# Seven block products for 15 of 22 up-projection pairs in one SwiGLU phase, and modulation tiles moved to the other three

## The chip, the cores and the metric

The kernel runs on one core of one Trainium2 chip. The metric is the device time of one execution in microseconds. TensorE is called PE here, VectorE DVE, ScalarE ACT, GpSimd POOL and SyncE, which issues the weight transfers, SP.

## What is computed

Two layers of a diffusion backbone over 256 latent and 256 context tokens, D = 1024. Each layer is a half-step SwiGLU, a token mixer and a second half-step SwiGLU; each of them is modulated with shift, scale and gate and wrapped in a layer norm. What matters here:

```python
def modulate(h, shift, scale): return h * (1.0 + scale) + shift
def post_norm(h, y, gate, res_w, g, b):
    return layer_norm(ALPHA * h + res_w * gate * y, g, b)
def swiglu(u, w_up, w_down):
    a, v = jnp.split(u @ w_up, 2, axis=-1)          # D_FF = 2816 columns each
    return (jax.nn.silu(a) * v) @ w_down
def ffn_sublayer(h, m, j, w_up, w_down, g, b):
    u = modulate(h, m[:, :, 3 * j], m[:, :, 3 * j + 1])
    return post_norm(h, swiglu(u, w_up, w_down), m[:, :, 3 * j + 2], FFN_RES_W, g, b)
...
m_lat = (s_lat @ w_ada[l] + b_ada[l])               # 9 modulation vectors per layer, for latents
m_ctx = (s_ctx @ w_ada[l] + b_ada[l])               # and for context
```

## The kernel before

Activations lie transposed, 128 channels on the partitions and all 512 tokens along a row (context in the left 256, latents in the right), so u is eight pages, each as a high part (uh, fp32r) and a low part (ul); two pages share a tile, hence the names u0 to u3. Every product is three fp32r matmuls (`mm3`, L370): high by high (L372), high by low (L373), low by high (L374).

Weights arrive in chunks of 512 KB, eight blocks of 128x128, in an order fixed beforehand. SP issues the transfer into one of three raw buffers wr (L255); ACT copies it into the high part wh (L342); DVE subtracts for the low part wl (L344). There are three split slots wh/wl. A chunk feeds 24 matmuls. A slot comes free when PE has used it; then ACT's next copy can begin.

The phases are called (layer, sub-layer): (0,0) is the first SwiGLU, (0,2) the second of layer 0, (1,0) the first of layer 1, which the change is about, and (1,2) the last, on the 256 latents alone. A SwiGLU phase (`ffn`) has an up projection of 22 pairs ft, a chunk of a and one of v, 24 matmuls each into a bank of 512. The first two pairs (three in (0,0)) are made while the layer norm before them brings the u pages one by one (`k_outer`, `ln_apply`: L676 makes u, L677 its low part). `act` takes a pair from the banks: silu on ACT (L760), product on DVE (L761), high part on ACT (L764), low part on DVE (L765). The hidden pages r are kept split. The down projection goes over eight output blocks, the last two in halves of the tokens (`tail`), so that the layer norm of half 0 overlaps with PE's work on half 1; L560 adds a finished block into the residual.

The modulation vectors are not made on PE: `ada_part` takes a 512 KB tile of w_ada through the same raw buffers, and DVE multiplies and accumulates it with two broadcast rows (L488, twice per tile) and adds the bias (L492). 128 tiles are spread over the SwiGLU phases, one in the middle of each chunk of the up projections and two per block of the down projections: 50 in (0,0), 52 in (0,2), 26 in (1,0).

Each engine executes its instructions in the order of a scheduler that works from the program's dependencies. Dependencies on a PSUM bank are kept for the bank as a whole.

## Time and profile before

| | us |
|---|---|
| median of three executions | 2721.28 |
| lowest, highest | 2720.58, 2723.74 |
| the profiled execution | 2722.64 |
| its span on the core | 2720.7 |
| PE busy in the span | 2659.9 |
| DVE busy | 1928.3 |
| ACT busy | 1222.9 |

The span is what the profiler sees from the first to the last instruction; 1.9 us of the execution lie around it. In the trace (0,0) runs from about 50 to 391 us, (0,2) from 1208 to 1577, (1,0) from 1577 to 1947 (its layer norm to 1603, its up projection to about 1822), and the last phase from 2507 to the end. The mixers lie between. In a timeline a row is one instruction or a run of equal ones: start, duration, engine, line, operation, output and inputs, shape, count; in brackets the idle time ahead of it and what ended it.

### The profile page before, as it was taken

To read this page: it belongs to the slowest core of one execution; us is meant where nothing else is said; L and a number is where in the kernel's file an instruction comes from. 1 tells how busy PE (TensorE), PEld (TensorE's weight loads), DVE (VectorE), ACT (ScalarE), POOL (GpSimd) and SP (SyncE) were. 2 spreads that over 40 slices of the span, in tenths; PEclk is the share of its full clock that TensorE was granted. 3 is DMA by queue.
4 is the path that set the end of the run, shared out by engine and by line. 5 is a ranking of instruction groups with operands and counts; after the bars stand their busy time and mean duration, and the time that the engine had idled before them with its cause. 6 is when DMAs were issued, how large, how long until landed. Compare 5 with 4: busy or idle time off the path is not lost.

```text
span 2720.7 us, 38673 instructions
## 1 busy us (share of the span) xinstructions
PE 2659.9 (98%) x14869; PEld 2280.2 (84%) x14869; DVE 1928.3 (71%) x3469; ACT 1222.9 (45%) x1755; POOL 353.8 (13%) x296
## 2 busy tenths in 40 slices
PE   9999999999999999999999999999998999999998
PEld 7888897778887888888888888888977898899997
DVE  5788769599877545468887588633697998676654
ACT  4323237963345344433323142332388745574543
POOL 0000132112121000040000130001312112012002
PEclk9999999999999999999999999999999999999999
DMA  7666534134343222235666446532333354343563
GB/s 280 193 189 200 172 122 130 60 99 149 105 134 109 78 86 78 88 99 170 194 195 191 132 129 199 169 120 97 108 123 105 111 174 150 107 142 124 175 191 116
DMA packets 117833, 380.49 MB, mean 140 GB/s; under 512 B 13888, under 2 KB 22352, under 8 KB 117648
## 3 DMA queue, kind: packets, MB, share of 16 engines
q1 hardware_dynamic: 116000, 373.52, 42.5%
q0 software_dynamic: 1504, 4.34, 0.5%
q8 instruction: 116, 1.90, 0.3%
q14 instruction: 69, 0.57, 0.1%
q10 hardware_dynamic: 144, 0.17, 0.0%
HBM read 373.63 MB, written 4.33 MB: 139 GB/s over the span
## 4 chain that ended last, share of the span: by engine, by line
PE 56%; DVE 7%; ACT 3%; issue 2%; DMA 1%; POOL 0%; SPq 0%; POOLq 0%; DVEq 0%; ACTq 0%
PE bank L372 17%; PE bank L373 17%; PE bank L374 17%; PE bank L1282 1%; PE bank L1262 1%; DVE wl L344 1%; DVE x L869 1%; DMA wr<-in_ws_dram 1%; DMA x<-acs_d 1%; DVE f L669 0%; DVE m1l L344 0%; ACT wh L342 0%; PE bank L921 0%; DVE f L670 0%; DVE f L676 0%
## 5 line engine op out<-in xcount | busy, mean ns | idle before, releaser
L342 ACT ACTIVATE wh<-wr 128x1024 fp32r<-128x1024 f32 x388 | 410.2, 1058 | 727.1 <-PE bank L373 493.2
L344 DVE TENSOR_TENSOR wl<-wr,wh 128x1024 fp32r<-128x1024 f32 x388 | 483.6, 1247 | 239.4 <-ACT wh L342 237.6
L488 DVE SCALAR_TENSOR_TENSOR ada_scr<-wr,sb 128x1024 f32<-128x1024 f32 x256 | 316.7, 1237 | 135.9 <-DMA wr<-in_ws_dram 133.2
L372 PE MATMUL bank<-u0h,wh 128*128 128x512 f32 (+1 forms) x660 | 247.1, 376 | 5.5 <-ACT u0h L675 3.8
L372 PE MATMUL bank<-r,wh 128*128 128x512 f32 (+1 forms) x736 | 251.3, 342 | 0.0
L374 PE MATMUL bank<-r,wl 128*128 128x512 f32 (+1 forms) x736 | 249.9, 340 | 0.0
L373 PE MATMUL bank<-r,wh 128*128 128x512 f32 (+1 forms) x736 | 249.7, 340 | 0.0
L374 PE MATMUL bank<-u0h,wl 128*128 128x512 f32 (+1 forms) x660 | 237.2, 360 | 3.9 <-DVE wl L344 3.9
L373 PE MATMUL bank<-u0l,wh 128*128 128x512 f32 (+1 forms) x660 | 236.2, 358 | 2.1 <-DVE u0l L677 2.0
L373 PE MATMUL bank<-u1l,wh 128*128 128x512 f32 (+1 forms) x660 | 235.1, 357 | 0.8 <-DVE u1l L677 0.7
L372 PE MATMUL bank<-u1h,wh 128*128 128x512 f32 (+1 forms) x660 | 233.5, 356 | 0.6 <-ACT u1h L675 0.6
L374 PE MATMUL bank<-u1h,wl 128*128 128x512 f32 (+1 forms) x660 | 234.0, 355 | 0.0
L372 PE MATMUL bank<-u2h,wh 128*128 128x512 f32 (+1 forms) x660 | 233.6, 355 | 0.0
L374 PE MATMUL bank<-u2h,wl 128*128 128x512 f32 (+1 forms) x660 | 233.4, 354 | 0.0
L373 PE MATMUL bank<-u2l,wh 128*128 128x512 f32 (+1 forms) x660 | 233.2, 354 | 0.0
L373 PE MATMUL bank<-u3l,wh 128*128 128x512 f32 (+1 forms) x644 | 228.6, 355 | 1.5 <-DVE u3l L677 1.5
L372 PE MATMUL bank<-u3h,wh 128*128 128x512 f32 (+1 forms) x644 | 228.3, 356 | 0.0
L374 PE MATMUL bank<-u3h,wl 128*128 128x512 f32 (+1 forms) x644 | 228.0, 354 | 0.0
L372 PEld LDWEIGHTS bank<-r,wh 128*128 128x128 f32 x736 | 139.4, 190 | 15.3 <-issue 0.3
L374 PEld LDWEIGHTS bank<-r,wl 128*128 128x128 f32 x736 | 139.5, 190 | 15.1
L373 PEld LDWEIGHTS bank<-r,wh 128*128 128x128 f32 x736 | 139.5, 190 | 14.8
L372 PEld LDWEIGHTS bank<-u0h,wh 128*128 128x128 f32 x660 | 125.6, 191 | 29.7 <-issue 5.6
(530 smaller groups left out, 5919.4 us busy)
## 6 DMA issues: line engine op xcount, KB each, us to landing
wr<-in_ws_dram SPq DMA_DIRECT2D x602, 512.0 KB, 4.0
m1r<-in_ws_dram SPq DMA_DIRECT2D x29, 512.0 KB, 3.9
ada<-in_ws_dram SPq DMA_DIRECT2D x16, 512.0 KB, 9.0
x<-acs_d SPq DMA_DIRECT2D x22, 256.0 KB, 3.4
x<-acs_d SPq DMA_DIRECT2D x39, 128.0 KB, 3.6
x<-in_lw_dram SPq DMA_DIRECT2D x16, 256.0 KB, 3.2
f<-acs_d SPq DMA_DIRECT2D x25, 128.0 KB, 3.4
sb<-s_d SPq DMA_DIRECT2D x6, 512.0 KB, 5.8
```

What stands on the lines that cost most here:

```text
L342: self.pin(nc.scalar.activation(hi, raw, AF.Copy))
L344: self.pin(nc.vector.tensor_tensor(lo, raw, hi, op=ALU.subtract))
L372: x = self.pin(nc.tensor.matmul(out, st[0], mv[0], start=start, stop=False, skip_group_check=True))
L373: self.pin(nc.tensor.matmul(out, st[0], mv[1], start=False, stop=False, skip_group_check=True))
L374: self.last_mm = self.pin(nc.tensor.matmul(out, st[1], mv[0], start=False, stop=stop, skip_group_check=True))
L488: nc.vector.scalar_tensor_tensor(self.ada_scr, raw.rearrange("p a b -> p (a b)"), 1.0, self.sb[b], op0=ALU.mult, op1=ALU.mult, accum_out=o ...
L869: nc.vector.scalar_tensor_tensor(ys[:, :, a:z], xs[:, :, a + o:z + o], w(k), ys[:, :, a:z], op0=ALU.mult, op1=ALU.add)
L1262: nc.tensor.matmul(ps[:, 0:256], cc(kt[d], a), vv(a), start=True, stop=True)
L1282: nc.tensor.matmul(cc(po[w], c), lh, rh, start=n == 0, stop=n == len(steps) - 1, skip_group_check=True)
```

## The change

In (1,0), pairs 0 to 3 stay as they were. Of the eighteen pairs 4 to 21, called p = 0 to 17, every sixth (p = 5, 11, 17) keeps its 48 matmuls of 512. The other fifteen are computed as a 2x2 by 2x2 product with seven block products: the weight pair (a and v by the even and the odd row blocks) and u (even and odd pages by left and right tokens) are each cut into 2x2, and seven products of 4 row blocks and 256 tokens, called (p,1) to (p,7), take the place of eight. Each is 12 matmuls of 128x256 into half a bank. The sums of weights are made on DVE (L426), and every sum is split anew into high and low part (L459 on ACT, L460 on DVE); the sums of u are made once (`columns`), and results are summed on DVE from the banks (L544, L546, L548). For this u itself is kept (`ucol`), written by the layer norm into a new tile. Hidden pages from ft = 8 on are kept unsplit in f32 and are split during the down projection's first block, and their low parts are copied to other pages behind it. Two further raw buffers serve (1,0).

No modulation tiles are left in (1,0). (0,0) has 63 (three per even pair up to 16, and a third per block in the down projection), (0,2) has 57, and the last phase has 8, one in every even pair.

```diff
+KSPLIT = (0, 2, 4, 6, 1, 3, 5, 7)
+NFULL = 8
+def products(n):
+    r, rest = [], []
+    for p in range(n):
+        last = p == n - 1
+        if p % 6 == 5:
+            r += [(p, 11)] + rest + [(p, 12), (p, 21), (p, 22)]
+            rest = []
+        else:
+            r += [(p, 1), (p, 7)] + rest + [(p, m) for m in ((6, 4, 5, 2) if last else (6, 4, 2, 5))]
+            rest = [(p, 3)]
+    return r + rest
...
+    def strassen_parts(self, i):
...
+            if m in (1, 7, 11, 21):
+                n = i + 2 * p + (m in (7, 21))
+                R[p, 1 if m in (1, 11) else 7] = self.raw_next(tuple(self.wlist[8 * n:8 * n + 8])), len(self.seq) - 1
...
+            elif m == 7:
+                R[p, 5] = self.F()
+                sub(R[p, 5], a21, a22, ALU.add)
+                sub(a21, a11, a21)
+                src = a21
+            elif m == 6:
+                sub(a11, R[p, 5], a11)
+                src = a11
...
+            nc.scalar.activation(flat(t.hi), src, AF.Copy)
+            nc.vector.tensor_tensor(flat(t.lo), src, flat(t.hi), op=ALU.subtract)
+            if m == 2:
+                R[p, 3] = self.F()
+                sub(R[p, 3], a12, a11)
...
+    def strassen(self, l, j, fts, finish):
...
+            if m == 1:
+                x_of[p], z_of[p], g_of[p], v_of[p] = self.B(), self.B(), self.F(), self.F()
+            X, Z, G, V = x_of[p][:, left], z_of[p], g_of[p], v_of[p]
+            out = Z[:, left] if m in (7, 4) else Z[:, right] if m == 2 else X
+            for b in range(4):
+                if m in (1, 2, 3):
...
+                y = self.mm3(out, (t.hi[:, b], t.lo[:, b]), mv, m in (1, 7) and b == 0, b == 3)
...
+            if m == 1:
+                nc.scalar.activation(G[:, left], X, AF.Copy)
+            elif m == 7:
+                nc.scalar.activation(V[:, right], Z[:, left], AF.Copy)
+            elif m == 6:
+                nc.scalar.activation(V[:, left], X, AF.Copy)
+            elif m == 5:
+                nc.scalar.activation(G[:, right], X, AF.Copy)
+                nc.vector.tensor_tensor(V[:, right], G[:, right], V[:, right], op=ALU.add)
+            elif m == 4:
+                nc.vector.tensor_tensor(V[:, left], Z[:, left], V[:, left], op=ALU.add)
+            elif m == 2:
+                nc.vector.tensor_tensor(G[:, left], Z[:, right], G[:, left], op=ALU.add)
+                nc.scalar.activation(G[:, left], G[:, left], AF.Silu)
+                self.fB(Z)
+            elif m == 3:
+                nc.scalar.activation(G[:, right], X, AF.Silu)
...
+    def columns(self):
...
+        for o, a, b in ((b11, b12, b11), (b12, b22, b12), (b22, b22, b11), (b21, b21, b22)):
+            self.behind(nc.vector.tensor_tensor(o, a, b, op=ALU.subtract), self.last_u)
...
             if nxt:
-                u = up[:, k % 2 * TL:(k % 2 + 1) * TL]
+                u = self.ucol[:, q, k % 2, s] if self.with_u else up[:, k % 2 * TL:(k % 2 + 1) * TL]
...
+            self.ucol = q.tile([P, KT // 2, 2, T], F32, name=f"uc{l}{jm}")
...
-                    if kt == KT // 2:
-                        self.ada_part()
+                    if kt == KT // 2 and not paired and (not c0 or i == 0 and ft % 2 == 0):
+                        self.ada_part(1 + (l == jm == i == 0 and ft % 2 == 0 and ft < 17))
...
+                else:
+                    nc.vector.tensor_tensor(pages[ft - NFULL], v, g, op=ALU.mult)
+                    hid.append(None)
+                    late.append(ft)
...
-                if ft in (8, 16):
+                if late:
+                    late_parts(2)
+                if not paired and not c0 and (ft in (8, 16) or ft == 12 and (m < 5 or not jm)):
                     self.ada_part()
```

On PE, in the middle of (1,0)'s up projection, one chunk ended and the next began like this before; a pair is 48 such matmuls of 512:

```order
L372 MATMUL bank3_119<-u3h_88,wh2_97 128x512
L373 MATMUL bank3_119<-u3l_89,wh2_97 128x512
L374 MATMUL bank3_119<-u3h_88,wl2_98 128x512
L372 MATMUL bank0_116<-u0h_82,wh1_95 128x512 [waits Activation_49]
L373 MATMUL bank0_116<-u0l_83,wh1_95 128x512
L374 MATMUL bank0_116<-u0h_82,wl1_96 128x512 [waits DVE_49]
```

After, in the pair p = 8: the last matmul of (8,4) into the left half of bank 3, nine matmuls of (8,5) into bank 6, then (8,2) into the right half of bank 3 (t100 and t103 are sums of u, split):

```order
L605 MATMUL bank3_119<-t103h_10934,wl2_98 128x256
L603 MATMUL bank6_122<-t100h_10928,wh1_95 128x256 [waits Activation_49]
L604 MATMUL bank6_122<-t100l_10929,wh1_95 128x256
L605 MATMUL bank6_122<-t100h_10928,wl1_96 128x256 [waits DVE_49]
L603 MATMUL bank6_122<-t100h_10928,wh1_95 128x256
L604 MATMUL bank6_122<-t100l_10929,wh1_95 128x256
L605 MATMUL bank6_122<-t100h_10928,wl1_96 128x256
L603 MATMUL bank6_122<-t100h_10928,wh1_95 128x256
L604 MATMUL bank6_122<-t100l_10929,wh1_95 128x256
L605 MATMUL bank6_122<-t100h_10928,wl1_96 128x256
L603 MATMUL bank3_119<-u0h_82,wh2_97 128x256 [waits DVE_49]
L604 MATMUL bank3_119<-u0l_83,wh2_97 128x256
```

Rows of 512-wide matmuls have become rows of 256-wide ones, and the first matmul of (8,2) now waits for a DVE operation on its bank, L546; the last three matmuls of (8,5) follow behind (8,2).

On DVE, a pair of (1,0) before had low parts, the hidden product and its low part, and the modulation tiles in between:

```order
L488 SCALAR_TENSOR_TENSOR ada_scr_10886,mods1_66<-wr1_91,sb0_10884 128x1024 [waits DMAHW7_49]
L761 TENSOR_TENSOR f5_104<-bank2_118,f5_104 128x512 [waits PE_49,Activation_49]
L344 TENSOR_TENSOR wl1_96<-wr0_90,wh1_95 128x1024 [waits DMAHW6_49,Activation_49]
L765 TENSOR_TENSOR r10_13_10853<-f5_104,r10_12_10852 128x512 [waits Activation_49]
L488 SCALAR_TENSOR_TENSOR ada_scr_10886,mods1_66<-wr1_91,sb1_10885 128x1024
L492 TENSOR_SCALAR mods1_66<-mods1_66,par1_64 128x2 [waits DVE_49]
L344 TENSOR_TENSOR wl0_94<-wr2_92,wh0_93 128x1024 [waits DMAHW0_49,PE_49,Activation_49]
```

After, the pair p = 8 from L546, for which PE's (8,2) waits; x10r1 is one of the two further raw buffers, hr10 a hidden page:

```order
L546 TENSOR_TENSOR f5_104<-bank3_119,f5_104 128x256 [waits PE_49,Activation_49]
L460 TENSOR_TENSOR wl2_98<-wr1_91,wh2_97 128x512 [waits Activation_49]
L548 TENSOR_TENSOR f6_105<-bank3_119,f6_105 128x256 [waits PE_49]
L460 TENSOR_TENSOR wl2_98<-x10r1_10947,wh2_97 128x512 [waits Activation_49]
L544 TENSOR_TENSOR f5_104<-f6_105,f5_104 128x256 [waits Activation_49]
L460 TENSOR_TENSOR wl1_96<-wr1_91,wh1_95 128x512 [waits PE_49,Activation_49]
L460 TENSOR_TENSOR wl1_96<-f0_99,wh1_95 128x512 [waits PE_49,Activation_49]
L426 TENSOR_TENSOR f0_99<-wr2_92 128x512 [waits DMAHW1_49,DVE_49]
L426 TENSOR_TENSOR wr2_92<-wr0_90,wr2_92 128x512 [waits DMAHW0_49,DVE_49]
L460 TENSOR_TENSOR wl0_94<-wr0_90,wh0_93 128x512 [waits PE_49,Activation_49]
L426 TENSOR_TENSOR wr0_90<-f0_99,wr0_90 128x512 [waits DVE_49]
L1036 TENSOR_TENSOR hr10_4_10944<-f5_104,f6_105 128x512 [waits Activation_49]
```

Two more low parts (L460) and one sum (L426), which waits for the L426 into wr0, follow, and then L546 of p = 9. The modulation tiles are gone from here, and fifteen short operations stand between one L546 and the next.

On DVE at the end of (0,2), before, u values and low parts of half 0 (L676, L677) stood ahead of the last residual tile (L560 from bank 7):

```order
L677 TENSOR_TENSOR u2l_87<-f0_99,u2h_86 128x256 [waits DVE_49,PE_49,Activation_49]
L669 TENSOR_TENSOR f1_100<-f8_107,f6_105 128x256 [waits Pool_49]
L670 TENSOR_TENSOR f1_100<-f1_100,f11_110 128x256 [waits DVE_49]
L676 TENSOR_SCALAR f0_99<-f1_100,gp0_68,gp1_69 128x256 [waits DVE_49]
L677 TENSOR_TENSOR u3l_89<-f0_99,u3h_88 128x256 [waits DVE_49,PE_49,Activation_49]
L560 SCALAR_TENSOR_TENSOR f7_106<-bank7_123,gp2_70,f7_106 128x256 [waits PE_49]
```

After (L791 is the residual tile now, L907 and L908 are u and its low part, uc10 is the new tile for u):

```order
L399 TENSOR_TENSOR wl0_94<-wr0_90,wh0_93 128x1024 [waits DMAHW6_49,PE_49,Activation_49]
L791 SCALAR_TENSOR_TENSOR f7_106<-bank7_123,gp2_70,f7_106 128x256 [waits PE_49]
L907 TENSOR_SCALAR uc10_10939<-f5_104,gp0_68,gp1_69 128x256
L822 TENSOR_TENSOR f0_99<-f7_106 128x256 [waits DVE_49]
L908 TENSOR_TENSOR u0l_83<-uc10_10939,u0h_82 128x256 [waits DVE_49]
L907 TENSOR_SCALAR uc10_10939<-f5_104,gp0_68,gp1_69 128x256
L907 TENSOR_SCALAR uc10_10939<-f10_109,gp0_68,gp1_69 128x256
L908 TENSOR_TENSOR u0l_83<-uc10_10939,u0h_82 128x256 [waits DVE_49]
```

The first five L907 and L908 have moved behind the last residual tile.

## Rows read from the trace of the kernel before

**Rows 1.** The page: busy us, share, instructions by engine; the chain that ended last.

```profile
PE 2659.9 (98%) x14869; PEld 2280.2 (84%) x14869; DVE 1928.3 (71%) x3469; ACT 1222.9 (45%) x1755; POOL 353.8 (13%) x296
...
PE 56%; DVE 7%; ACT 3%; issue 2%; DMA 1%; POOL 0%; SPq 0%; POOLq 0%; DVEq 0%; ACTq 0%
```

**Rows 2.** Windows: length, busy us of PE, PEld, DVE, ACT, POOL; clock; DMA.

```profile
60.00:260.00 200.00, 200.00 (x885) 165.58 (x884) 162.07 (x264) 59.63 (x74) 0.00 (x0) 1.00 0.61 191
...
1577.00:1603.00 26.00, 24.49 (x191) 23.28 (x191) 23.73 (x55) 13.58 (x19) 15.31 (x11) 1.00 0.24 76
1610.00:1740.00 130.00, 130.00 (x576) 107.62 (x575) 105.19 (x168) 38.38 (x48) 0.00 (x0) 1.00 0.61 194
1750.00:1830.00 80.00, 80.00 (x355) 66.24 (x354) 29.32 (x31) 27.04 (x33) 0.00 (x0) 1.00 0.31 106
...
2530.00:2640.00 110.00, 110.00 (x919) 110.00 (x918) 63.39 (x80) 52.79 (x79) 0.00 (x0) 1.00 0.59 187
```

**Rows 3.** The same window for line L488 alone: DVE's busy time and entries.

```profile
1610.00:1740.00 130.00, 59.12 (x96) 1.00 0.61 194
```

**Rows 4.** Timeline of PE in (1,0)'s up projection, 29 matmuls left out between.

```profile
1619.85 0.39 PE L374 MATMUL bank<-u0h,wl 128*128 128x512 f32 x1
...
1626.65 0.39 PE L374 MATMUL bank<-u1h,wl 128*128 128x512 f32 x1
```

**Rows 5.** Timeline of PE in the last phase, 26 matmuls left out between.

```profile
2599.73 0.28 PE L373 MATMUL bank<-u3l,wh 128*128 128x256 f32 x1
...
2602.97 0.28 PE L373 MATMUL bank<-u3l,wh 128*128 128x256 f32 x1
```

**Rows 6.** Timeline of DVE in (0,2): 512-wide operations in a row.

```profile
1474.32 0.69 DVE L576 TENSOR_TENSOR f<-f,f 128x512 f32<-128x512 f32 x1
1474.92 4.30 DVE L578 SCALAR_TENSOR_TENSOR f<-f,f 128x512 f32<-128x512 f32 x7
```

**Rows 7.** Timeline of DVE in the norm before the last phase: 256-wide in a row.

```profile
2507.99 0.42 DVE L639 SCALAR_TENSOR_TENSOR f<-bank,f 128x256 f32<-128x256 f32 x1 [0.35 <-ACT f L638]
2508.34 1.42 DVE L669 TENSOR_TENSOR f<-f,f 128x256 f32<-128x256 f32 x4
```

**Rows 8.** Timeline of the last phase: a copy and its low part, a group's end.

```profile
2557.26 1.06 ACT L342 ACTIVATE wh<-wr 128x1024 fp32r<-128x1024 f32 x1 [1.51 <-issue]
...
2558.35 1.23 DVE L344 TENSOR_TENSOR wl<-wr,wh 128x1024 fp32r<-128x1024 f32 x1 [1.32 <-ACT wh L342]
...
2560.01 0.28 PE L372 MATMUL bank<-u0h,wh 128*128 128x256 f32 x1
...
2560.28 0.42 DVE L761 TENSOR_TENSOR f<-bank,f 128x256 f32<-128x256 f32 x1 [0.70 <-PE bank L374]
```

**Rows 9.** Timeline of DVE in the norm of (1,0): L676 reads L670's result.

```profile
1574.70 0.42 DVE L670 TENSOR_TENSOR f<-f,f 128x256 f32<-128x256 f32 x1
1575.16 0.41 DVE L676 TENSOR_SCALAR f<-f,gp,gp 128x256 f32<-128x256 f32 x1
```

**Rows 10.** Groups of ACT by line and shape, 1200 to 1960: busy us, mean ns.

```profile
L764 ACT ACTIVATE r<-f 128x512 fp32r<-128x512 f32 x44 | 27.7, 632 | 70.6 <-DVE f L761 70.6
...
L637 ACT ACTIVATE f<-bank 128x256 f32<-128x256 f32 x6 | 2.3, 384 | 31.3 <-PE bank L635 31.3
```

**Rows 11.** Timeline of DVE around the end of (0,2).

```profile
1564.85 0.82 DVE L676 TENSOR_SCALAR f<-f,gp,gp 128x256 f32<-128x256 f32 x2
...
1569.89 0.97 DVE L677 TENSOR_TENSOR u1l<-f,u1h 128x256 fp32r<-128x256 f32 x1
...
1575.85 0.43 DVE L677 TENSOR_TENSOR u3l<-f,u3h 128x256 fp32r<-128x256 f32 x1 [0.28 <-ACT u3h L675]
1576.42 0.48 DVE L560 SCALAR_TENSOR_TENSOR f<-bank,gp,f 128x256 f32<-128x256 f32 x1
...
1578.91 0.42 DVE L639 SCALAR_TENSOR_TENSOR f<-bank,f 128x256 f32<-128x256 f32 x1 [1.46 <-ACT f L638]
```

**Rows 12.** Transfers of weights, 60 to 260: count, KB, median us to landing.

```profile
wr<-in_ws_dram SPq DMA_DIRECT2D x74, 512.0 KB, 4.3
```

225 lines of the change are left out of this document (211 added, 14 removed).

## The prediction

> **What bounds the kernel now.** I read the page first. PE is busy for 2659.9 us of a span of 2720.7, DVE for 1928.3, and 56% of the chain that ended last is PE, with DVE next at 7% [rows 1]. So the kernel as a whole is bound by TensorE, and a share of 71% on DVE says nothing yet about single stages. Next the windows, stage by stage [rows 2]. In the up projections (60:260, 1610:1740, 2530:2640) and in the down projection (1750:1830) PE is busy in every microsecond; only in the layer norm at 1577:1603 is it busy for 24.49 of 26.00 us, while DVE is busy for 23.73 of them. Fewer TensorE microseconds in the stage at 1610:1740 therefore shorten the kernel one for one, as long as DVE and ACT bring the operands in time, and lost time in the norm is DVE's. In 1610:1740 DVE is at 105.19 of 130 us (81%), of which 59.12 us are the modulation tiles [rows 2, 3]. The change takes these away and puts sums in their place.
>
> **Removed: TensorE time.** In the stage that changes, thirty 512-wide matmuls take from 1619.85 to 1626.65, 0.2267 us from one start to the next [rows 4]. Twenty-seven 256-wide ones of the last phase take from 2599.73 to 2602.97, 0.120 each [rows 5]. In both stages the granted clock was 1.00, the upper level of 2.4 GHz [rows 2]. A pair of up blocks is 48 of the first kind, 10.88 us; as seven block products it is 84 of the second kind, 10.08 us. That is 0.80 us for each of 15 pairs, **12.0 us** in all. Three pairs of the eighteen stay as they are. The gain per pair is small because half-wide matmuls cost 53% of a full one, and the saved eighth of the arithmetic is halved by it.
>
> The Trainium skill has a rule that promises more: "TensorE: Matmul & The Clock Gate", section "Wait — 56ns, not 53.3ns?", states a start-to-start time of N over 2.4 GHz plus about 2.5 ns. By it a pair would go from 10.35 to 9.17 us, 17.7 us for the fifteen, and the time below would be 2708. The trace disagrees with it for these fp32r products (0.2267 and 0.120), and the sum goes by the trace.
>
> **Added: DVE's loop in a block pair.** For one pair DVE makes twelve 128x512 operations (four weight sums, seven low parts, one product) and three of 128x256 from the banks, in place of two L344, L761, L765 and the modulation tiles. In a row of 512-wide operations one starts 0.602 us after another ((4.30−0.69)/6), though one alone takes 0.69 [rows 6]; 256-wide ones start 0.333 apart ((1.42−0.42)/3) [rows 7]. Busy: 12×0.602+3×0.333 = 8.2 us of 10.08, no more than DVE's 81% before. What matters is the order. In the new PE order of a pair, (p,2)'s first matmul waits for DVE: it writes the right half of a bank whose left half L546 reads after (p,4). Nine matmuls of (p,5), 1.08 us, stand between. Call the end of (p,4) zero. (p,2) ends at 1.08+1.44 = 2.52. DVE's L548 reads its result; a bank's last matmul to DVE's read of it took 0.27 us (group's end 2560.01, L761 at 2560.28) [rows 8], so L548 starts at 2.79. From it to the next pair's L546 there are 11 operations of 0.602 and two of 0.333 in DVE's order, 7.29 us, so L546 could start at 10.08, just when the next (p,4) ends. Three of the eleven wait for the operation right before them. Such a wait makes a 256-wide one start 0.46 us after the other instead of 0.333 [rows 9]: +0.12 each, 0.36. Low parts whose high part ACT copies late cost more: the copy takes 0.63 us and hands on within 0.03 (ACT ends at 2558.32, DVE starts at 2558.35) [rows 8, 10]. I take 0.25 for all of them, between nothing and two whole copies (1.3). So L546 starts 0.6 us after (p,4), takes 0.42, and with a hand-over of some 0.1 the wait ends at 1.1 to 1.2 against a cover of 1.08: **0.12 us** per loop. There are four such loops in each of the three runs of five block pairs, 12 in all: 1.4 us lost. A full pair between the runs (10.88 us on PE and little on DVE) lets DVE catch up, but at the pair behind it only five matmuls of (p,5) stand ahead of the wait, so I add 0.2 twice, and 0.3 for the first pair, which comes right after the column sums: 0.7. The bounds of this part are 0 (all covered) and what rival C gives.
>
> ACT has seven copies of 0.63, four of 0.38 from a bank and two silus (an estimate from the copies: 0.4) per pair [rows 10], 6.7 us of 10.08, and is not the bound. POOL does nothing there [rows 2].
>
> **Added: the norm ahead of it.** Before, five of half 0's u values and low parts (L676, L677) are made while PE is still in the last half of the down projection's tail: the first pair at 1564.85, the last L677 at 1575.85, and only then comes the last residual tile L560 at 1576.42 [rows 11]. After, these ten operations stand behind it (L907, L908), because the new column page lies in memory from which PE's tail still reads hidden pages. That adds 10×0.333 = 3.3 us to DVE in a stage in which it has 2.3 us free and PE already stands idle for 1.5 [rows 2]. But the first of them come while the statistics are on PE and ACT (idle 1.46 us before L639 at 1578.91) [rows 11], and not every k is late. Bounds 0 and 3.5; I take **2.0**, nearer to the upper, since DVE is busy for 91% there.
>
> **Moved: modulation tiles.** A tile is two L488 with their accumulator reads, 59.12/24 = 2.46 us [rows 3], and a small L492 behind them; I take 2.66. In (0,0), two pairs of up blocks with the extra tile hold 5 tiles, four L344 (1.23 less the same overlap of 0.08 [rows 6, 8]), two L761 and two L765: 5×2.66+4×1.15+4×0.602 = 20.3 us of DVE for 21.76 of PE. It fits; if each took 0.1 us more it would be 21.7, and with 0.2 more PE would lose about 0.3 seven times, 2 us. Nine transfers in 21.76 us over three buffers leave 7.25 us for each buffer, with 4.3 to land [rows 12]. In the last phase two blocks take 11.52 us; 2.66 more on DVE (58% before) is 81%, and five transfers instead of four leave 6.9 us per buffer against about the same 4.3 (187 GB/s there, 191 in (0,0)) [rows 2, 12]. The lead of a low part follows from rows 8: with three split slots the one that ends at 2559.58 belongs to the row of blocks behind the one that PE starts at 2560.01, which takes 24×0.120 = 2.88 us, so it is 3.3 us early. In (0,0) a row takes 24×0.2267 = 5.44, and by the same steps (2×5.44 less 2.45 for the hand-over, the copy and the low part) it is up to 8.4 early. One more tile ahead of a low part takes 1.3 to 2.7 of either. I take 0.5 us for all of it, between 0 and 5 (2 in (0,0), 8×0.4 at the end). The down projections of (0,0) and (0,2) take their tiles while DVE is at 37% or less of a down stage (29.32 of 80) [rows 2]: nothing. Late splitting of the hidden pages and the 14 copies in the down projection lie under the same cover; without it they would cost their first wait only, about 1 us.
>
> **Sum.** −12.0+1.4+0.7+2.0+0.5 = −7.4 us. The profiled run took 2722.64 us (span 2720.7 and 1.9 around it), which would become 2715.2; the median is 1.36 lower, 2721.28, and becomes **2714**.
>
> **Rivals.** B: all waits are covered, and the whole 12 us come: 2709. For it: PE waits for nearly nothing in the stages of today. Against: the loop above fills the pair to the last tenth.
>
> C: DVE's loop, not PE, paces the block pairs. The cover is 1.08 us, so every further tenth in the loop comes out at the end 12 times. If the low parts lose 0.8 us per pair in place of 0.25, the loop is 10.8 us, the loss grows by 12×0.55 = 6.6, and the time is **2720.5**, no change. For it: eleven operations in a row, seven of which need ACT's copy first; against: ACT has a third of its time free.
>
> D, the slower side: DVE's operations don't overlap here as in rows 6, because they alternate between results of ACT, banks and each other. Then 13 operations start a full 0.685 or 0.42 after one another, 0.08 more each, 1.1 us per loop; 12×1.1 = 13.2 us more, and with 3.5 in the norm the time is 2714+13.2+1.5 = **2729**. It decides from about 0.11 us more per operation than I count, or 0.08 together with the norm. For it: in the norm, single 256-wide operations take up to 0.97 us [rows 11]; against: there POOL works beside them, and in this stage it does not [rows 2].
>
> The Trainium skill has a rule that speaks for D: "VectorE: DVE Perf Modes", section "The DRAIN you can't avoid", says that the next operation does not start until the pipe of the one before is empty; by it the time is D's. Rows 6 show starts 0.08 us before the end of the one before, so the trace doesn't bear the rule out for a plain row; no stretch here shows the new mixture.
>
> E: the moved tiles bind in (0,0) or the last phase, at 4 us more: 2718.
>
> **How the numbers follow.** A (my forecast, 2711 to 2717.5) 0.47, B 0.09, C 0.24, D 0.12, E 0.08. What the measurement can tell from no change is 0.2%, 5.4 us: faster means below 2715.9, slower above 2726.7. Most of A and all of B are faster (0.40+0.09, and 0.01 of E): 0.50. The rest of A, C and most of E are the same: 0.36. D and a tail of C are slower: 0.14. The range takes in B at its lower end (2709) and C with the norm's bound (2720.5+1.5+2): 2709 to 2724; what is left out is D and little else.
>
> **What would show it.** In the new profile PE's busy time in the pairs falls by 12 us plus what it waits; 256-wide matmuls start 0.120 apart; before (p,2) PE waits about 0.1 us for L546 in most pairs. Waits of 0.5 us or more there mean C; DVE starts of 0.685 apart mean D. In the norm PE's idle time grows from 1.5 to some 3.5 us, the releaser being L908. If PE waits at the low parts L344 in (0,0) or the last phase, E. The prediction is wrong if 256-wide matmuls of this stage don't reach 0.120, or if PE waits elsewhere than at these places.

## The result and the profile after

The changed kernel takes 2739.74 us (median of six, 2736.22 to 2742.19) against 2722.51 for the kernel before (six, 2718.73 to 2725.79): ratio 1.0067, 95% interval 1.0056 to 1.0078. It is 17 us slower, where 2714 was forecast and 2724 was the end of the range.

The page of the kernel after, its busy times and the chain that ended last, answering to [rows 1]:

```profile
span 2734.0 us, 40229 instructions
...
PE 2656.8 (97%) x15409; PEld 2297.4 (84%) x15409; DVE 2027.5 (74%) x3663; ACT 1284.8 (47%) x1929; POOL 353.0 (13%) x296
...
PE 51%; DVE 9%; ACT 4%; DMA 3%; issue 2%; POOL 1%; DVEq 0%; POOLq 0%; ACTq 0%; SPq 0%
```

PE is busy for only 3.1 us less and idle for 16.4 us more (2734.0−2656.8 against 2720.7−2659.9). To see where, one instruction that both kernels have was taken as a mark: the statistics of each norm on DVE (L639 before, L870 after). How much later than before it starts in the profiled execution, cumulative, in us (called the shift below):

| end of (the norm behind) | (0,0) | mixer 0 | (0,2), half 0 | (0,2), half 1 | (1,0) | mixer 1 | last |
|---|---|---|---|---|---|---|---|
| changed kernel | +10.0 | +9.3 | +10.8 | +12.0 | +6.6 | +8.5 | +13.2 |

So (0,0), in which no product was changed, lost 10.0 us, (0,2) 1.5, the last phase 4.7, and the mixers 1.2 together. The stage with the seven products, from (0,2)'s half 0 to (1,0)'s norm, gained 4.2 us. Each shift is read from one execution: over all the runs below, mixer 0 and mixer 1, which no edit touches, move by −2.6 to +3.3 us in it, so a shift of one or two microseconds counts only where a wait in the trace goes with it.

**(0,0).** PE's waits there, after:

```profile
PE bank L803 <- DVE f L791: 7.1, 1, 7.1
PE bank L604 <- DVE u0l L908: 1.6, 1, 1.6
PE bank L605 <- DVE wl L399: 1.5, 4, 0.5
```

and the same wait before (waits of PE, same stretch):

```profile
PE bank L572 <- DVE f L560: 0.4, 1, 0.4
```

L803 is the small product of `res_mean` in the second block of the down projection: it needs the first block's residual tile (L791). It waited 0.4 us before and 7.1 now. The timeline of DVE after shows what stood ahead of that tile (some rows left out):

```profile
281.72 1.22 DVE L719 SCALAR_TENSOR_TENSOR ada_scr<-wr,sb 128x1024 f32<-128x1024 f32 x1
...
284.39 1.22 DVE L719 SCALAR_TENSOR_TENSOR ada_scr<-wr,sb 128x1024 f32<-128x1024 f32 x1
...
286.80 1.22 DVE L399 TENSOR_TENSOR wl<-wr,wh 128x1024 fp32r<-128x1024 f32 x1
...
288.07 1.22 DVE L719 SCALAR_TENSOR_TENSOR ada_scr<-wr,sb 128x1024 f32<-128x1024 f32 x1
...
289.22 0.48 DVE L791 SCALAR_TENSOR_TENSOR f<-bank,gp,f 128x256 f32<-128x256 f32 x1
...
290.75 0.48 DVE L791 SCALAR_TENSOR_TENSOR f<-bank,gp,f 128x256 f32<-128x256 f32 x1
```

Three tiles (the first halves are shown; the second half of the third, at 289.61, lies between the two residual operations) stand ahead of it, and DVE came to the first of them only at 281.72. Before, two tiles stood there, and DVE came to the first at 276.34:

```profile
276.34 1.23 DVE L488 SCALAR_TENSOR_TENSOR ada_scr<-wr,sb 128x1024 f32<-128x1024 f32 x1
...
283.54 0.48 DVE L560 SCALAR_TENSOR_TENSOR f<-bank,gp,f 128x256 f32<-128x256 f32 x1
```

PE then shows a second loss, in its timeline behind the wait and in the window around it (columns: length, busy time of PE, PEld, DVE, ACT and POOL with counts, granted clock, DMA share, GB/s):

```profile
283.80 0.39 PE L605 MATMUL bank<-r,u3l 128*128 128x512 f32 x1
291.29 2.07 PE L803 MATMUL bank<-f,ones 128*128 128x512 f32 x2 [7.10 <-DVE f L791]
292.37 1.42 PE L603 MATMUL bank<-r,u3h 128*128 128x512 f32 x1
293.58 0.63 PE L604 MATMUL bank<-r,u3h 128*128 128x512 f32 x1
294.01 0.63 PE L605 MATMUL bank<-r,u3l 128*128 128x512 f32 x1
```

```profile
283.00:300.00 17.00, 9.90 (x30) 6.96 (x29) 16.61 (x33) 4.41 (x5) 0.00 (x0) 0.70 0.56 183
```

After standing still for 7.1 us, PE makes 512-wide matmuls at 0.43 us instead of 0.2267 [rows 4], the lower level of 1.2 GHz, for some eight of them. The granted clock is 0.50 in the stretch 287 to 297; over the window shown, of 17 us, the mean is 0.70.

**Why DVE was late.** In the up projection PE lost 1.0 us in 200:

```profile
60.00:260.00 200.00, 198.96 (x874) 163.40 (x873) 172.11 (x288) 56.61 (x71) 0.00 (x0) 1.00 0.63 203
```

But the low parts slip: one and the same low part starts at 217.26 before and at 225.16 after. From 235 us to the end of the up projection, where no pair has a third tile any more, each of them is still 6.0 to 6.5 us later than before.

```profile
217.26 1.22 DVE L344 TENSOR_TENSOR wl<-wr,wh 128x1024 fp32r<-128x1024 f32 x1
```

```profile
224.01 1.23 DVE L719 SCALAR_TENSOR_TENSOR ada_scr<-wr,sb 128x1024 f32<-128x1024 f32 x1 [1.23 <-DMA wr<-in_ws_dram]
...
225.16 1.22 DVE L399 TENSOR_TENSOR wl<-wr,wh 128x1024 fp32r<-128x1024 f32 x1
```

DVE still has idle time there: by its groups in 60 to 260 it waits 21.2 us for transfers of tiles, while the low part behind the tile has to wait as well. It waited longer before, 31.5 us, so the waiting alone does not explain the slip; experiments below separate transfers and work. Before, then after:

```profile
L488 DVE SCALAR_TENSOR_TENSOR ada_scr<-wr,sb 128x1024 f32<-128x1024 f32 x73 | 89.3, 1223 | 32.4 <-DMA wr<-in_ws_dram 31.5
...
L719 DVE SCALAR_TENSOR_TENSOR ada_scr<-wr,sb 128x1024 f32<-128x1024 f32 x85 | 103.9, 1223 | 22.1 <-DMA wr<-in_ws_dram 21.2
```

**The pairs of (1,0).** PE and DVE at (p,2) of a pair, after:

```profile
1718.85 0.28 PE L605 MATMUL bank<-t100h,wl 128*128 128x256 f32 x1
1719.21 0.39 PE L603 MATMUL bank<-u0h,wh 128*128 128x256 f32 x1
1719.43 0.28 PE L604 MATMUL bank<-u0l,wh 128*128 128x256 f32 x1
1719.55 0.28 PE L605 MATMUL bank<-u0h,wl 128*128 128x256 f32 x1
```

```profile
1716.93 0.69 DVE L460 TENSOR_TENSOR wl<-wr,wh 128x512 fp32r<-128x512 f32 x1
1717.53 0.68 DVE L460 TENSOR_TENSOR wl<-f,wh 128x512 fp32r<-128x512 f32 x1
1718.13 0.68 DVE L426 TENSOR_TENSOR f<-x10r 128x512 f32<-128x512 f32 x1
1718.73 0.42 DVE L546 TENSOR_TENSOR f<-bank,f 128x256 f32<-128x256 f32 x1
1719.07 0.68 DVE L460 TENSOR_TENSOR wl<-x10r,wh 128x512 fp32r<-128x512 f32 x1
1720.95 0.42 DVE L548 TENSOR_TENSOR f<-bank,f 128x256 f32<-128x256 f32 x1 [1.20 <-PE bank L605]
```

The wait for L546 is where it was forecast. It costs 0.24 us in this pair, and then the first matmul behind it takes 0.22 instead of 0.12. Over the 1260 matmuls of the fifteen pairs the steps are 0.12 as in [rows 5], and everything above that (and above 0.2267 for the wide ones) sums to 4.3 us. Some 3.4 of it is at (p,2). The other 0.9 is in four pairs of the first run of five, where the first matmul of (p,5) waits for ACT's L541, which copies the result of (p,6) out of the same half bank. A pair's loop on DVE has fifteen operations, so in a plain pair fourteen stand between one L546 and the next.

**The norm.** On DVE, after, the u writes follow the last residual tile, behind an idle stretch of 5 us:

```profile
1588.17 0.48 DVE L791 SCALAR_TENSOR_TENSOR f<-bank,gp,f 128x256 f32<-128x256 f32 x1 [4.96 <-PE bank L605]
1588.57 0.40 DVE L907 TENSOR_SCALAR uc<-f,gp,gp 128x256 f32<-128x256 f32 x1
...
1589.23 0.42 DVE L908 TENSOR_TENSOR u0l<-uc,u0h 128x256 fp32r<-128x256 f32 x1
```

Counted the same way as the pairs, PE's steps above 0.12 and 0.2267 from 15 us before the last residual tile to the first block pair sum to 7.2 us, and to 3.8 before: 3.4 more, 0.8 of them still ahead of that tile. PE's longest wait there is for a low part of u, after and then before:

```profile
PE bank L604 <- DVE u1l L908: 1.6, 1, 1.6
...
PE bank L373 <- DVE u3l L677: 1.2, 2, 1.0
```

### The profile page after: what moved, and what is told of

Same layout as the page of the kernel before. It is cut to its first block, busy times and chain, and to the rows that moved or that the text cites. A ratio compares the mean times of both kernels' runs of the same rounds, so it can differ in the third digit from the quotient of the medians.

```text
span 2734.0 us, 40229 instructions
## 1 busy us (share of the span) xinstructions
PE 2656.8 (97%) x15409; PEld 2297.4 (84%) x15409; DVE 2027.5 (74%) x3663; ACT 1284.8 (47%) x1929; POOL 353.0 (13%) x296
## 4 chain that ended last, share of the span: by engine, by line
PE 51%; DVE 9%; ACT 4%; DMA 3%; issue 2%; POOL 1%; DVEq 0%; POOLq 0%; ACTq 0%; SPq 0%
PE bank L603 16%; PE bank L604 15%; PE bank L605 15%; DMA wr<-in_ws_dram 2%; DVE wl L399 1%; PE bank L1575 1%; PE bank L1555 1%; ACT wh L397 1%; DVE x L1162 1%; DVE f L900 1%; DVE wl L460 1%; DVE m1l L399 0%; DVE f L901 0%; ACT x L1215 0%; DVE ada_scr L719 0%
## 5 line engine op out<-in xcount | busy, mean ns | idle before, releaser
L397 ACT ACTIVATE wh<-wr 128x1024 fp32r<-128x1024 f32 x351 | 370.5, 1057 | 648.1 <-PE bank L604 317.0
L399 DVE TENSOR_TENSOR wl<-wr,wh 128x1024 fp32r<-128x1024 f32 x351 | 439.5, 1254 | 202.5 <-ACT wh L397 200.9
L603 PE MATMUL bank<-r,wh 128*128 128x512 f32 (+1 forms) x678 | 232.1, 343 | 0.0
L605 PE MATMUL bank<-r,wl 128*128 128x512 f32 (+1 forms) x678 | 230.3, 340 | 0.0
L604 PE MATMUL bank<-r,wh 128*128 128x512 f32 (+1 forms) x678 | 230.1, 340 | 0.0
L603 PE MATMUL bank<-u1h,wh 128*128 128x512 f32 (+1 forms) x645 | 223.0, 348 | 0.6 <-ACT u1h L906 0.6
L605 PE MATMUL bank<-u1h,wl 128*128 128x512 f32 (+1 forms) x645 | 223.5, 347 | 0.0
L604 PE MATMUL bank<-u3l,wh 128*128 128x512 f32 (+1 forms) x629 | 218.1, 347 | 0.6 <-DVE u3l L908 0.6
L605 PE MATMUL bank<-u3h,wl 128*128 128x512 f32 (+1 forms) x629 | 217.5, 346 | 0.0
L826 POOL TENSOR_TENSOR f<-f,f 128x512 f32<-128x512 f32 (+1 forms) x6 | 7.6, 1260 | 1095.0 <-DVE f L791 1095.0
L605 PEld LDWEIGHTS bank<-u0h,wl 128*128 128x128 f32 x645 | 122.8, 190 | 28.8 <-DVE wl L399 13.3
L604 PEld LDWEIGHTS bank<-u0l,wh 128*128 128x128 f32 x647 | 123.5, 191 | 20.5 <-issue 5.2
```

What stands on the lines that cost most here:

```text
L397: self.pin(nc.scalar.activation(hi, raw, AF.Copy))
L399: self.pin(nc.vector.tensor_tensor(lo, raw, hi, op=ALU.subtract))
L603: x = self.pin(nc.tensor.matmul(out, st[0], mv[0], start=start, stop=False, skip_group_check=True))
L604: self.pin(nc.tensor.matmul(out, st[0], mv[1], start=False, stop=False, skip_group_check=True))
L605: self.last_mm = self.pin(nc.tensor.matmul(out, st[1], mv[0], start=False, stop=stop, skip_group_check=True))
L826: nc.gpsimd.tensor_tensor(self.acc[:, s], self.hp[0][:, s], h[:, s], op=ALU.add)
```

## The experiments

The theory at this point: the moved tiles cost 16 us, mostly in (0,0), and the products gain 4. The rival: the tiles are harmless, as the prediction's sum had it, and products and norm cost the time.

### The two halves of the change apart

`tiles_only` is the kernel before with the tiles spread as after:

```diff
-                    if kt == KT // 2:
-                        self.ada_part()
+                    if kt == KT // 2 and not (l == 1 and jm == 0) and (not c0 or i == 0 and ft % 2 == 0):
+                        self.ada_part(1 + (l == jm == i == 0 and ft % 2 == 0 and ft < 17))
```

(and the same condition in the down projection).

> The kernel before with one part of the change: the modulation tiles spread as in the changed kernel (63, 57, none in (1,0), 8 in the last phase), all products as before. Theory T (the moved tiles bind): the shifts read from the profile of the changed kernel come here too, +10 us by the end of (0,0), +1.5 in (0,2), +4.7 in the last phase, so about 2738 against 2722. Rival P (the seven products and the norm ahead of them cost the time, the tiles next to nothing, as the prediction's sum had it with 0.5 us): about 2723.

2737.14 against 2720.95, ratio 1.0059 (1.0044 to 1.0074); shifts +11.4 by the end of (0,0), +1.6 in (0,2), +3.0 in the last phase.

`products_only`: the changed kernel with the old places, and `ada_until` writing the bias alone for the tiles left over:

```diff
         while self.ada_q and self.ada_q[0] < (l, j + 1):
-            self.ada_part()
+            la, ja, ka = self.ada_q.pop(0)
...
+                self.nc.vector.tensor_scalar(self.mods[la][:, ja, ka, b:b + 1], self.par[la][:, c:c + 1], 1.0, None, op0=ALU.mult)
```

> The changed kernel with the tiles at their old places in (0,0) and (0,2) (50 and 52) and the other 26 left out altogether (no transfer, no DVE product, the bias alone stands in their place), so the seven products and the norm stand alone. T: what the profile shows for (1,0), -5.4 us, and +1.2 at the end of (0,2): about 2718, 4 us below before. P: the loss is in these parts: 2735 or more. If the prediction's other terms were all right, it would be -7.9: 2714.6.

2716.75 against 2720.95, ratio 0.9988 (0.9979 to 0.9998). The rival is out: the tiles alone cost 16 us, and products and norm gain 4. The two do not quite add up to the change, 12 us against 17 by the medians. The shifts do add up in (0,0) (11.4−0.5 against 10.0), (0,2) and (1,0) (−5.4 in both); in the last phase they give 2.9 against 4.7.

### What in (0,0) makes DVE late

`no_up_extra` leaves out the second tile of the even pairs in (0,0)'s up projection:

```diff
-                        self.ada_part(1 + (l == jm == i == 0 and ft % 2 == 0 and ft < 17))
+                        self.ada_part()
```

> The changed kernel without the seven further tiles of (0,0)'s up projection (left out: no transfer, no DVE product); the third tile per block of the down projection stays. If the backlog that makes DVE 5.4 us late at the end of the up projection comes from these seven, PE's wait for the first residual tile (7.1 us) falls to 1 to 2.5, the slow-clock stretch behind it goes, and the time is 6 to 8 us below the changed kernel, about 2732. If the third tile of the first block alone makes the wait, little changes: 2738.

2724.17, ratio 1.0011 (1.0001 to 1.0020), some 8 us below what was expected; shift at the end of (0,0) +0.2 in place of +10.0. PE's wait for the residual tile:

```profile
PE bank L807 <- DVE f L795: 0.9, 1, 0.9
```

`no_early_third` leaves out the third tile in the first two blocks of the down projections:

```diff
-                if not paired and not c0 and (ft in (8, 16) or ft == 12 and (m < 5 or not jm)):
+                if not paired and not c0 and (ft in (8, 16) or ft == 12 and m > 1 and (m < 5 or not jm)):
```

> The changed kernel without the third modulation tile in the first two blocks of the down projections of (0,0) and (0,2) (four tiles left out), the rest as changed. If one tile of 2.7 us in the first block stands ahead of the residual tile on DVE, the wait of 7.1 us in (0,0) falls to about 4.4, that of 1.1 in (0,2) to nothing, and the time to about 2735 (2733 if the clock does not fall). If the up projection's backlog makes it all: 2739.

2732.64, ratio 1.0046 (1.0029 to 1.0063); shift by (0,0) +8.4, in (0,2) nothing more (+1.5 before). The wait:

```profile
PE bank L807 <- DVE f L795: 5.5, 1, 5.5
```

So in (0,0) the seven tiles of the up projection make the loss; the third tile ahead of the residual tile adds 1.6. In (0,2), where DVE comes in time, it makes the whole of PE's wait for that tile, 1.1 us, which is gone in this run. The rest of (0,2) is not so firm: with the same tiles there, no_up_extra's execution lost 3.7 us in that phase.

Is it DVE's time or the transfers? For the second tile of a place, one run keeps DVE's work and drops the transfer, the other the reverse:

`products_no_transfer` (DVE multiplies the broadcast row by itself, times 0):

```diff
-        for l, j, k in self.ada_q[:n]:
+        for i, (l, j, k) in enumerate(self.ada_q[:n]):
+            o = self.mods[l][:, j, k, :]
+            if i:
+                for b in range(2):
+                    nc.vector.scalar_tensor_tensor(self.ada_scr, self.sb[b], 0.0, self.sb[b],
+                                                   op0=ALU.mult, op1=ALU.mult, accum_out=o[:, b:b + 1])
...
+                continue
```

`transfer_no_products` (DVE reads two columns of the tile and lets the buffer go):

```diff
             raw = self.raw_next((("adb", l, j, k),))
-            o = self.mods[l][:, j, k, :]
+            if i:
+                nc.vector.tensor_scalar(o, raw[:, 0, 0:2], 1.0, None, op0=ALU.mult)
+                self.raw_done()
+                continue
```

> The changed kernel, but the seven further tiles of (0,0)'s up projection have no transfer: DVE's two products and the bias stay, made on the broadcast row that is there already (times 0). Theory D (DVE's time is what runs out, 20.3 of 21.76 us by the count, and the row of tiles holds the low parts up): nothing is gained, about 2738. Theory B (three raw buffers run out: a tile holds one for its landing, its wait and its 2.5 us of products): the low parts come in time as without these tiles, about 2725.

> The changed kernel, but of the seven further tiles of (0,0)'s up projection only the transfer stays: DVE reads two columns of each in place of the two products. Theory D: 2725, as without the tiles. Theory B in its strict form (the transfers alone are too many): 2738; if it is the holding of a buffer by DVE's products: between, 2726 to 2732.

2725.23 (ratio 1.0025, 1.0015 to 1.0034) without the transfers, 2735.36 (1.0058, 1.0043 to 1.0073) without the products; shifts at the end of (0,0) +1.8 and +10.2. The waits, in this order:

```profile
PE bank L810 <- DVE f L798: 3.6, 1, 3.6
```

```profile
PE bank L807 <- DVE f L795: 7.2, 1, 7.2
```

The transfers alone make the whole loss. DVE's 19 us of products alone make a small part of it: 1.6 us by the shift, 2.7 by the wait for the residual tile, 3.8 by the ratios. An even pair has five transfers in 10.88 us, 6.5 us for each turn of three buffers; landing takes 4.1 of that, and what is left has to hold the wait for the engine in order and its reading. The tile that comes late holds up the low part behind it.

That the buffers run out, and not the rate of the transfers, is read from the trace: in 60 to 260 of the changed kernel SP stands for 176 of the 200 us waiting until DVE has read a buffer, and a transfer takes no longer to land than before (4.1 us in the median, 4.3 in [rows 12]). No run gave (0,0) a fourth buffer, so this last step is not shown by an experiment.

### The last phase

`no_last` leaves out the eight tiles of the last phase:

```diff
-                    if kt == KT // 2 and not paired and (not c0 or i == 0 and ft % 2 == 0):
+                    if kt == KT // 2 and not paired and not c0:
```

> The changed kernel without the eight tiles of the last phase (left out: no transfer, no DVE product). Theory T (they cost the 3 to 5 us by which the last phase grew in the traces with them): 2735 against 2739.7, and the shift of the last phase's norm against the kernel before goes from +4.7 to 0. Rival (that phase is longer for what precedes it): 2739.

2730.07, ratio 1.0039 (1.0025 to 1.0053). The shift of the last phase is −0.8 in place of +4.7. In the changed kernel PE waits there for low parts and their high parts:

```profile
PE bank L605 <- DVE wl L399: 2.5, 3, 1.0
...
PE bank L603 <- ACT wh L397: 1.2, 2, 0.7
```

The times of this run and of no_up_extra lie further below the changed kernel (8 and 15 us by the ratios) than the shifts of the stages in question say (5.5 and 10), and the two halves fell 5 us short of it. The profiled execution of the changed kernel took 2736.22 us, 3.5 less than the median of its six, and lies 13.6 above the profiled one before, which is near the 12 of the halves. Where the rest of the 17 us, 4 to 5, is lost stays open.

### The wait in the pairs

From here to the end of the next section the runs stand on products_only, without the 26 tiles. `products_own_bank`:

```diff
-            out = Z[:, left] if m in (7, 4) else Z[:, right] if m == 2 else X
+            out = Z[:, left] if m in (7, 4) else W[:, right] if m == 2 else X
...
-                nc.vector.tensor_tensor(G[:, left], Z[:, right], G[:, left], op=ALU.add)
+                nc.vector.tensor_tensor(G[:, left], W[:, right], G[:, left], op=ALU.add)
```

(W is a bank of its own.)

> The products alone as in the run of that name (2716.7), with (p,2) writing into a bank of its own instead of the other half of (p,4)'s bank, so that its first matmul does not wait for DVE's L546. Theory W (the 14 waits and the slower matmul behind each, 4.3 us in the trace, come from that bank alone, and DVE has time left in the pair): about 2712.5. Rival (DVE's loop fills the pair, and the wait moves to the low parts): 2716 to 2717.

2712.57 against 2719.32, ratio 0.9974 (0.9964 to 0.9984), 3.8 us below the products alone by the ratios (the kernel before took 2720.95 beside that run). The window 1640 to 1800, after and in this run:

```profile
1640.00:1800.00 160.00, 159.61 (x1220) 153.32 (x1219) 127.61 (x214) 88.56 (x188) 0.00 (x0) 1.00 0.30 101
```

```profile
1640.00:1800.00 160.00, 160.00 (x1247) 156.07 (x1246) 128.10 (x217) 95.81 (x201) 0.00 (x0) 1.00 0.30 105
```

27 matmuls more in the same 160 us, and DVE at 80%: PE's excess over the pairs is 0.1 us in place of 4.3. DVE's loop had time; the shared bank made PE wait for it. The waits at (p,5) are gone too: (p,2) now follows (p,4) directly, and (p,5) comes after it.

### The norm

`u_later` lets the norm write u where it did before, and adds it again for the differences:

```diff
-        self.with_u = paired
+        self.with_u = False
...
+            for k in range(KT):
+                self.behind(nc.vector.tensor_tensor(self.ucol[:, k // 2, k % 2], self.uh[k], self.ul[k], op=ALU.add), self.last_u)
             self.columns()
```

> The products alone with a bank of their own (2712.6), with u not kept by the norm but added again on DVE from its high and low parts after the norm (eight operations of 128x512), so that the norm's u writes go to the pages they went to before. If the 1.2 us at the end of (0,2) and some 2 in the norm come from the writes that had to stand behind the last residual tile, both go: the first norm's shift stays where it was (+0.0 between its two halves in place of +1.2), and PE's lost time in the norm falls from 4.9 to about 2.8 us. What the eight additions (4.8 us of DVE) cost behind it, as the low parts of the third pair stand behind them: 0 to 5. So 2709 to 2714 by this; if the writes are not the cause, +1.2 stays.

2720.28, ratio 1.0000 (0.9991 to 1.0009). The shift between the two halves of the norm is 0.0 in place of +1.2, and PE's excess in the norm is 3.4 us in place of 7.2. But the third pair waits for its low parts, which stand behind the additions: PE loses 10.9 us there, part of it at the lower clock. Waits of PE from 1570 to 1860 in this run:

```profile
PE bank L601 <- DVE wl L399: 6.1, 1, 6.1
PE bank L599 <- ACT wh L397: 2.4, 1, 2.4
```

`products_norm_free` puts the additions behind the third pair's code and the differences behind the fourth's, and starts the block pairs at the sixth:

```diff
-        reg = 4 if paired else NFT
-        self.with_u = paired
+        reg = 5 if paired else NFT
+        self.with_u = False
...
-        if paired:
-            self.columns()
...
             act(*pp)
+            if paired and ft == 2:
+                for k in range(KT):
+                    self.behind(nc.vector.tensor_tensor(self.ucol[:, k // 2, k % 2], self.uh[k], self.ul[k], op=ALU.add), self.last_u)
+            if paired and ft == 3:
+                self.columns()
```

> The products alone with a bank of their own (2712.6), 17 pairs of which the third of six stay full (the fifth pair stays regular), u added again on DVE after the third pair's low parts are under way and its differences made after the fourth, so that no weight's low part waits behind all of it. If the norm's u writes cost 3.7 us (PE's lost time in the norm 7.2 us with them, 3.4 in the run u_later) and what u_later lost (10.9 us at the third pair) was the low parts behind the additions: -3.7, +0.8 for one block pair less or none, so 2709 to 2711. If the additions cost what the writes cost: 2713 or more.

2710.04, ratio 0.9964 (0.9952 to 0.9976): 2.5 us below products_own_bank in time, 3.8 by the shift from (0,2)'s half 0 to (1,0)'s end (−12.2 against −8.4). PE's excess in the norm is 3.5 in place of 7.2. So the u writes cost 2.5 to 3.8 us; as times alone, the two runs' intervals overlap. The −12.2 is also what the products were forecast to give once nothing waits for them.

### Other places for the 26 tiles

All parts are computed from here on, (p,2) has its own bank, and no up projection has a further tile. In `both`, eight stand in the down projections of (0,0) and (0,2) and 18 in (1,0)'s own, with the vectors `sb` loaded again there:

```diff
+                if (m and ft in (8, 13, 18) or 2 <= m <= 4 and ft == 3) if paired else \
+                        not c0 and (ft in (8, 16) or ft == 12 and m > 1):
                     self.ada_part()
...
+            self.sb = [q.tile([P, D], F32, name=f"sc{l}{jm}{b}") for b in range(2)]
+            for b in range(2):
+                nc.gpsimd.dma_start(self.sb[b], self.s_d[b:b + 1].to_broadcast([P, D]))
```

> All parts computed: the changed kernel with (p,2) in a bank of its own, and the 26 tiles at other places: none further in any up projection, none in the last phase; a third tile per block of the down projections of (0,0) and (0,2) from block 2 on (8), and 18 in (1,0)'s own down projection from its second block on. If a tile costs nothing where no low part or residual tile that PE waits for stands behind it: 2712 to 2714, the time of the products alone with the bank of its own. If further tiles cost wherever they stand: 2718 or more.

2721.31, ratio 1.0006 (0.9996 to 1.0015). Free in (0,0) and (0,2) (shift −1.0 there), but (1,0)'s down projection loses 6.4 us: the sums of the norm wait for POOL, which waits for the last residual tiles:

```profile
PE bank L850 <- POOL f L824: 4.7, 1, 4.7
```

`both_early` moves tiles of the last block forward:

```diff
-                if (m and ft in (8, 13, 18) or 2 <= m <= 4 and ft == 3) if paired else \
-                        not c0 and (ft in (8, 16) or ft == 12 and m > 1):
+                if (1 <= m <= 4 and ft in (8, 13, 18) or 2 <= m and ft == 3 or m == 5 and ft == 8) if paired else \
+                        not c0 and (ft in (8, 16) or ft == 12 and m > 1 or ft == 4 and m == 3 and jm == 0):
```

> All parts computed: as the run both (2721.3), but in (1,0)'s down projection no tile stands behind ft = 8 of the last full block, and one more is in (0,0)'s down projection. In the trace of both the tiles in that block held up the residual tile that the sums of the norm wait for (PE waits 4.7 us for POOL, and its clock falls behind it), 6.4 us lost in that phase. If that is the cause: 2714 to 2715, between 2.5 and 3.5 in a thousand below the kernel before. If the tiles in (1,0)'s down projection cost by their number: 2719 or more.

2720.57, ratio 1.0005 (0.9997 to 1.0014), still 4.3 lost there.

`all_pairs` is both_early with block products in the three pairs that had none:

```diff
-        if p % 6 == 5:
+        if p < 0:
```

> As both_early, with all eighteen pairs as block products instead of fifteen. If DVE has time left in a pair once (p,2) has a bank of its own, three more pairs give 3x0.8 = 2.4 us: 2712. If DVE needs the full pairs to catch up, PE waits for low parts and the time is that of both_early or above it.

2720.86, ratio 1.0005 (0.9996 to 1.0014). Up to the second block of (1,0)'s down projection the shift is −10.6 against −7.9 for both_early, 2.7 better, as the three pairs should give; behind it 6.9 are lost.

`thin` leaves the last block without tiles:

```diff
-                if (1 <= m <= 4 and ft in (8, 13, 18) or 2 <= m and ft == 3 or m == 5 and ft == 8) if paired else \
-                        not c0 and (ft in (8, 16) or ft == 12 and m > 1 or ft == 4 and m == 3 and jm == 0):
+                if (2 <= m <= 4 and ft in (3, 8, 13, 18) or m == 1 and ft in (8, 12, 16, 20)) if paired else \
+                        not c0 and (ft in (8, 16) or ft == 12 and 1 <= m <= 4 or ft == 4 and m == 2):
```

> All parts computed: the changed kernel with the bank of its own, and the 26 tiles without any in the last full block of a down projection: ten in the down projections of (0,0) and (0,2) (a third in blocks 1 to 4, a fourth in block 2), 16 in (1,0)'s in blocks 1 to 4 (four each). If what the runs both and both_early lost in (1,0)'s down projection (6.4 and 4.3 us) comes from DVE being late at the last residual tiles, the block without tiles lets it catch up: 2713 to 2715. If four tiles per block are too many for three raw buffers wherever they stand: 2718 to 2721.

2718.58, ratio 0.9998 (0.9989 to 1.0007), 5.1 lost: not the last block's tiles, then.

`best` puts three edits shown above into one kernel: the places of thin, the norm of products_norm_free and `p < 0` of all_pairs.

> All parts computed: thin, with u added after the third pair as in products_norm_free and all 17 pairs from the sixth on as block products. If the parts add up: thin less 3.7 for the norm and less 1.6 for two more block pairs, 2708 to 2710, 4 in a thousand below the kernel before. If DVE has no time left without full pairs or in the down projection: 2715 or more.

2710.65, ratio 0.9967 (0.9955 to 0.9978): it adds up nearly (2708 to 2710 were expected), and 4.7 are still lost in that down projection. Waits, best:

```profile
PE bank L850 <- POOL f L824: 2.7, 1, 2.7
```

`three_per_block` is best with four tiles fewer in (1,0) and four more in the first two phases:

```diff
-                if (2 <= m <= 4 and ft in (3, 8, 13, 18) or m == 1 and ft in (8, 12, 16, 20)) if paired else \
-                        not c0 and (ft in (8, 16) or ft == 12 and 1 <= m <= 4 or ft == 4 and m == 2):
+                if (1 <= m <= 4 and ft in (8, 13, 18)) if paired else \
+                        not c0 and (ft in (8, 16) or ft == 12 and 1 <= m <= 4 or ft == 4 and 2 <= m <= 4):
```

> All parts computed: as the run best (2710.7), with three tiles per block in place of four in (1,0)'s down projection (12 in blocks 1 to 4) and the other four in the down projections of (0,0) and (0,2) (a fourth in blocks 2 to 4). If the 4.7 us that best still loses in (1,0)'s down projection come from four tiles per block on three raw buffers: 2706 to 2707. If any tile there costs: no change, 2710; if a fourth tile per block costs in (0,0) and (0,2) as it did in (1,0): above 2712.

2706.13, ratio 0.9950 (0.9937 to 0.9964), 14 to 15 us below the kernel before, with all of its output. The shift stays at −14.9 through that down projection, and the longest waits from 1540 to 1960 are these:

```profile
PE bank L600 <- DVE u3l L904: 1.2, 2, 1.0
PE bank L599 <- DVE x L1167: 0.6, 1, 0.6
PE bank L599 <- ACT u1h L902: 0.4, 1, 0.4
```

Sixteen tiles in (1,0)'s down projection, four per block, cost 4.7 us; twelve, three per block, cost nothing that shows. Whether the number in a block decides, or the places that went with it, was not separated. In (0,0) and (0,2), this kernel has four in blocks 2 to 4 and nothing is lost, so the number is not the same everywhere; what differs in (1,0) (POOL's additions and the copies of the low parts are candidates) was not tried.

## Why the prediction was wrong

**The products: right.** 12.0 us by 0.2267 and 0.120 per matmul; the 256-wide step in the new stage is 0.120, and products_norm_free, where neither of the added waits is left, gained 12.2. The rule of the Trainium skill weighed there ("TensorE: Matmul & The Clock Gate", section "Wait — 56ns, not 53.3ns?") is not borne out in this stage either.

**DVE's loop: right in place, a term too small.** The wait was foreseen at (p,2), with 2.1 us for all pairs; it was 4.3. The term left out the slower matmul behind each wait, 0.1 us, which [rows 4, 5] could not show, and the 0.9 us at (p,5), where PE waited for ACT; and waits were a little longer. Rivals C and D did not come: DVE's operations start 0.60 apart in the new mixture too (1716.93, 1717.53, 1718.13, 1718.73), 0.08 before the one ahead has ended. The section of the Trainium skill that was cited for D ("VectorE: DVE Perf Modes", "The DRAIN you can't avoid") says in the same paragraph that a next operation that is not held starts earlier; the prediction left that half out, and the trace agrees with it.

**The norm: right in mechanism, too small.** 2.0 was taken between 0 and 3.5; PE's excess grew by 3.4, near the upper bound, and its longest wait there, 1.6, is for L908, as forecast.

**The moved tiles: the step that failed.** They were priced at 0.5 us, 5 at most, and cost 16 (tiles_only). The prediction had said that it is wrong if PE waits at a place it does not name; the 7.1 us at the residual tile are such a place. Four things in that step were wrong.
- "Nine transfers in 21.76 us over three buffers leave 7.25 us for each buffer, with 4.3 to land" is a mean over two pairs. The change puts three tiles into one pair: 6.5 us per turn. And 4.3 to land is not the turn; the buffer is held until ACT and DVE, which take things in order, have read it. The low parts slipped by up to 8 us, nearly all of the lead of 8.4 that the prediction gave for this phase.
- "One more tile ahead of a low part takes 1.3 to 2.7 of either" counted the slip as if it were given back at each pair. It added up over seven pairs, and in the five pairs after them 6 us of it were still there.
- The upper bound was too low by its own count. Thirteen operations with 0.2 us more each make 20.3 into 22.9 us for the 21.76 of PE: 1.1 us, not 0.3, in each of seven places, 8 us and not 2.
- The down projection was called free since DVE is at 37% [rows 2]. A slip of 5 us and a third tile there stood ahead of the first block's residual tile, which PE needs 18 matmuls, 4.1 us, into the second block. That wait was already 0.4 us before: no cover was left. The share of busy time of a stage said nothing about it; the list of PE's waits in (0,0) did, and the prediction made no use of it.

On top came the lower clock behind the 7.1 us, which no term held: the prediction took the granted clock as given, because no wait in its sum was long.

Rival E named the right work and the right phases, with 4 us and a chance of 0.08, but looked for the wait at the low parts, where (0,0) lost 1.5 us. The last phase's part of it (8×0.4 = 3.2 as an upper bound) was near: 4.7 in the changed kernel, 3.0 in tiles_only.

## What to carry to other kernels

Work that is moved to an engine with idle time is free only if nothing that somebody waits for stands behind it in that engine's order: look up each such wait in the stage where the work goes, and how much slack it has, before counting shares. For transfers through few buffers count the turn of a buffer (landing, waiting, reading) in the densest stretch, not the mean. Where PE waits for another engine because two results share a bank, give the second its own bank before giving up the saving.

## What was not expected of the hardware

- A matmul behind a wait of a few tenths of a microsecond starts a step of 0.22 us instead of 0.12 (256 wide): the wait costs 0.1 more than its length.
- DVE and POOL slow each other at times. In both_early the 241 L715 with no POOL operation beside them take 1.21 to 1.23 us; of the 15 that overlap with one, eight take 2.19 to 2.31. In the rows below POOL's addition, 1.29 us in the kernel before, takes 2.27.

```profile
1880.62 2.19 DVE L715 SCALAR_TENSOR_TENSOR t103l<-wr,sc 128x1024 fp32r<-128x1024 f32 x1
```

```profile
1879.46 2.27 POOL L824 TENSOR_TENSOR f<-f,f 128x512 f32<-128x512 f32 x1 [12.89 <-DVE mods L719]
```
